# Four RMS norms of a decoder trunk take their inverse root as a power on 256 columns in GpSimd, in place of a power on 2 columns and a spreading matmul

## The chip, the cores and the metric

The kernel runs on one core of one Trainium2 chip. The metric is device time in microseconds (us). The kernel before takes 2422.91 us, the median of three runs that lie between 2422.68 and 2423.42. All times of single instructions come from one more execution, taken with the hardware profiler.

## The reference, cut to what matters

The program is a decoder trunk with two layers, 256 tokens and 2048 features, all in float32. Each layer is a token mixer, a gated MLP and an input embedding with a gate. Each of these three starts with an RMS norm, and a last norm ends the trunk: seven norms in all.

```python
def rmsnorm(x, g):
    x32 = x.astype(jnp.float32)
    y = x32 * lax.rsqrt(jnp.mean(x32 * x32, axis=-1, keepdims=True) + RMS_EPS)
    return (y * g.astype(jnp.float32)).astype(x.dtype)
...
    for i in range(DEPTH):
        a = rmsnorm(h, attn_norm[i])
...
        h = h + conv_ffn(rmsnorm(h, ffn_norm[i]), w_up[i], conv_w[i], conv_b[i], w_down[i])
        gate = jax.nn.sigmoid(rmsnorm(h, ple_norm[i]) @ w_ple_gate[i])
        h = h + gate * (p[i] @ w_ple[i])
    return rmsnorm(h, final_norm)
```

The change touches the norms with ffn_norm and ple_norm, two in each layer.

## The kernel before, in words

Activations lie with features on the 128 partitions and tokens on the 256 columns. Weights are streamed from HBM in groups of up to 1 MB (tile wr, three buffers) and cut into **units**. A unit is mostly 512 rows by 256 columns of a weight matrix. ScalarE casts it to the matmul's type (line 176) and VectorE takes the rest that the cast lost (line 177); both halves lie in one of four buffers named w. TensorE then issues 24 matmuls for the unit (line 215), each 128x256: 4 blocks of rows, 2 blocks of columns, and three products of halves. Four units make one result tile (psu, psg, pso and so on) in PSUM. The function `unit` keeps three units split ahead (LOOK = 3). As w has four buffers, the cast of unit k+4 waits until the matmuls of unit k have read theirs.

The order of the work comes from a counter. `tick` runs after each unit, and `defer(n, fn)` places a function n ticks later in the program; a scheduler then decides the order on each engine, which is fixed before the program runs. Each engine takes its instructions strictly in that order.

**The norm.** The gain of a norm is put on the activations at once (`norm_parts`), but the factor of each token, one over the root of the mean square, is put on the results of the matmuls later. So the matmuls after a norm don't wait for it. While h is completed, `norm_squares` adds up the squares of the features in a tile acc, 128 partitions by two halves of 256 tokens. `norm_finish` then defers two functions:

- `norm_sums` three ticks later: acc's two halves are added on VectorE (line 299), two matmuls with acc as weights and two columns of ones sum over the partitions (line 303, tile nps), so that the tokens come to lie on the partitions, 128 in each of two columns. VectorE divides by 2048 and adds epsilon (line 306, tile nv), and GpSimd raises the 128x2 numbers to the power -0.5 (line 308, tile rT; the exponents lie in a tile root).
- `norm_rows` five ticks later: VectorE and ScalarE each scale an identity matrix by a column of rT (lines 316 and 318, tile nd), a matmul of ones with these diagonals spreads the factors over all partitions (line 319, tile rps, 128x256), and VectorE copies them to SBUF (line 322, tile rb).

After that the factor is used: in the MLP the convolution starts with u = psu times rb (line 627 on VectorE), then comes a ScalarE instruction on u (line 630) and four VectorE instructions (line 633). In the embedding's gate it is gt = psg times rb (line 710), a sigmoid on ScalarE (line 711) and two more VectorE instructions (lines 712 and 713). `with_rows` puts these uses behind `norm_rows`. The norm in front of a mixer also needs rT itself, since the values v are scaled with tokens on the partitions, and a tile rq.

Counted from the start of the first product after a norm, TensorE's order is: units 1 to 3, nps, units 4 and 5, rps, units 6, 7, 8 and so on. Units 1 to 4 fill the first result tile, 5 to 8 the second.

Of the kernel before, what the change touches and what calls it, by code (L numbers as in the profile page):

```python
# [14 lines left out]
ALU = mybir.AluOpType  # L15
AX = mybir.AxisListType

P = 128
D = 2048
S = 256  # L20
# [10 lines left out]
EPS = 1e-6  # L31
SCALE = DH ** -0.5
# [72 lines left out]
def trunk(ctx: ExitStack, tc: tile.TileContext, xT, pT, pos, gains, conv, bf, cst, wst, out):  # L105
    nc = tc.nc
# [16 lines left out]
    acc = cpool.tile([P, 2, S], F32, name="acc")  # L123
    rb = cpool.tile([P, S], F32, name="rb")
    rq = cpool.tile([P, S], F32, name="rq")
    rT = cpool.tile([P, 2], F32, name="rT")

    root = cpool.tile([P, 2], F32, name="root")
# [3 lines left out]
    ones = ct[:, C_ONE:C_ONE + 128]  # L132

    def mm_tile(name):
        return psum.tile([P, 2, S], F32, name=name, tag="mm", bufs=4)

    def at_tile(name):
        return psum.tile([P, 2, 512], F32, name=name, tag="at", bufs=2)

    def t2_tile(name, shape=(P, 2, S), dt=F32):  # L140
        return work.tile(list(shape), dt, name=name, tag="t2", bufs=6)
# [52 lines left out]
    def defer(n, fn):  # L194
        later.append((at["tick"] + n, fn))
# [114 lines left out]
    def norm_rows(mixer):  # L310

        dg = t2_tile("nd", (P, 2, P))
        ps = at_tile("rps")
        for t in range(2):
            if t == 0:
                nc.vector.tensor_scalar_mul(out=dg[:, t, :], in0=ident, scalar1=rT[:, t:t + 1])
            else:
                nc.scalar.activation(out=dg[:, t, :], in_=ident, func=AF.Copy, scale=rT[:, t:t + 1])
        nc.tensor.matmul(ps[:, 0, :S], lhsT=ones, rhs=dg, start=True, stop=True)
        if mixer is None:  # L320
            return ps[:, 0, :S]
        nc.vector.tensor_copy(out=rb, in_=ps[:, 0, :S])
        if mixer:
            nc.vector.tensor_scalar_mul(out=rq, in0=rb, scalar1=SCALE)

    def norm_finish(mixer, sums=3, rows=5):
        at["rows"] = at["tick"] + rows
        defer(sums, norm_sums)
        defer(rows, lambda: norm_rows(mixer))

# [317 lines left out]
    for l in range(DEPTH):  # L648
        st = {}
        if l == 0:  # L650
            split_unit()
            rest_of_start()
            for op in range(8):
                if op in (2, 4, 6):
                    for i in (op - 2, op - 1):
                        norm_parts(i, 0, X)
                ple_up(0, op)
            defer(1, lambda: norm_parts(6, 0, X))
            defer(2, lambda: norm_parts(7, 0, X))
            constants()  # L660
            for i in range(8):
                defer(3 + i, lambda i=i: norm_squares(i, tc.keep_in_program_order))
            norm_finish(True, 12, 14)
# [11 lines left out]

        staggered("pso", Y, "w_out", l, _cuts(KT), out_done)
        norm_finish(False)
        for b, (g0, g1) in enumerate(BLOCKS):
            for g in range(g0, g1):
# [7 lines left out]

            staggered("psd", Y, "w_down", l, _cuts(2 * (g1 - g0)), down_done, 2 * g0, 2 * g0)
        norm_finish(False)
        if l + 1 < DEPTH:  # L690
            praw = load_p(l + 1)
# [7 lines left out]
        for op in range(8):  # L699
            end = l + 1 == DEPTH and op == 7  # L700
            if end:
                ws = [unit("w_ple_gate", l, 4 * i, op * 256)[1] for i in range(4)]
                ps = [at_tile("pse")[:, j, :S] for j in range(2)]
            else:
                ps = mm_tile("psg")
# [15 lines left out]
            else:  # L721
                more = []
                for j in range(2):
                    for k in range(KT):
                        for n, (a, b) in enumerate(((0, 0), (0, 1), (1, 0))):
                            nc.tensor.matmul(ps[j],  # L726
                                             lhsT=ws[k // 4][:, k % 4, a, j * P:(j + 1) * P],
                                             rhs=X[:, k, b, :], start=k == 0 and n == 0,
                                             stop=k == KT - 1 and n == 2)
# [14 lines left out]
    assert not later and at["unit"] == len(UNITS)  # L744
    norm_sums(more)
    rps = norm_rows(None)
    for k0, k1 in ((0, 1), (1, 2), *((k, k + 2) for k in range(2, KT, 2))):
        hs = h[:, k0:k1, :]
# [79 lines left out]
```

## Time and profile before

| what | value |
|---|---|
| three runs, median (lowest to highest) | 2422.91 us (2422.68 to 2423.42) |
| the profiled execution, its own time | 2423.48 us |
| span in its profile | 2421.7 us |
| busy share of TensorE matmuls, VectorE, ScalarE | 99%, 65%, 51% |
| busy time of GpSimd | 5.8 us in 13 instructions |
| memory traffic | 458 MB, 189 GB/s mean |

The span is what the profile covers; 1.8 us of the execution's own time lie outside of it. In a timeline row, the first number is the start in us from the beginning of the span, the second the duration of the row in all, then engine, line, operation, the tiles written and read with their shapes, the count, and in brackets how long the engine had been idle and who released it. PE is TensorE's matmuls, PEld its weight loads, DVE VectorE, ACT ScalarE, POOL GpSimd. A float32 matmul shows up as two matmul records, a fp32r one as one.

### The profile page before, as it was taken

Reading aid. Unit: us, or ns where it says so; the run is one execution under the profiler, and the core shown is the slowest. Engines: PE = TensorE matmul, PEld = TensorE weight load, DVE = VectorE, ACT = ScalarE, POOL = GpSimd, SP = SyncE. Lnnn points to the kernel's source line nnn. Section 1 sums busy time; section 2 is a strip of 40 time slices with the busy share of each in tenths; the row PEclk is TensorE's granted clock in tenths of the full one; section 3 lists DMA queues with packets and bytes.
Section 4 is the critical chain, followed back from the end, with each engine's and each line's share of the span. In section 5 each row is a group of like instructions: output and inputs, shape, how many; then the busy total and the mean of one; then the engine's idle time right before and its main releaser. Section 6 shows DMA issues by size and latency. Waiting matters only on the chain.

```text
span 2421.7 us, 47927 instructions
## 1 busy us (share of the span) xinstructions
PE 2407.1 (99%) x20992; PEld 2401.0 (99%) x20992; DVE 1581.5 (65%) x2066; ACT 1227.9 (51%) x1546; POOL 5.8 (0%) x13
## 2 busy tenths in 40 slices
PE   9999999999999999999999999999999999999998
PEld 9999999999999999999999999999999999999997
DVE  7666766776567657767755555667665776567666
ACT  6554455554355445555554444555544554455554
POOL 0000000000000000000000000000000000000000
PEclk9999999999999999999999999999999999999999
DMA  7454455555555555555555454555555555555553
GB/s 285 166 181 172 174 182 192 192 192 194 197 197 196 187 197 192 193 186 202 184 188 173 167 181 163 199 190 194 192 192 193 192 196 191 201 194 187 186 202 122
DMA packets 66818, 458.05 MB, mean 189 GB/s; under 512 B 7552, under 2 KB 7840, under 8 KB 16944
## 3 DMA queue, kind: packets, MB, share of 16 engines
q1 hardware_dynamic: 66576, 454.93, 53.3%
q8 instruction: 164, 2.69, 0.4%
q14 instruction: 46, 0.38, 0.0%
q0 software_dynamic: 32, 0.06, 0.0%
HBM read 452.86 MB, written 2.10 MB: 188 GB/s over the span
## 4 chain that ended last, share of the span: by engine, by line
PE 99%; DVE 0%; DMA 0%; ACT 0%; issue 0%; SPq 0%; POOLq 0%; DVEq 0%; ACTq 0%
PE psu L215 40%; PE psd L215 20%; PE psk L215 7%; PE psq L215 7%; PE pso L215 7%; PE psv L249 7%; PE psg L215 7%; PE avp L529 1%; PE psv L262 0%; PE psp L215 0%; PE pse L726 0%; PE scs L482 0%; PE sps L517 0%; PE avp L526 0%; DMA h<-in_x 0%; PE scs L480 0%
## 5 line engine op out<-in xcount | busy, mean ns | idle before, releaser
L177 DVE TENSOR_TENSOR w<-wr,w 128x1024 fp32r<-128x1024 f32 (+2 forms) x874 | 1045.6, 1198 | 687.2 <-ACT w L176 683.2
L176 ACT CAST w<-wr 128x1024 fp32r<-128x1024 f32 (+2 forms) x874 | 900.9, 1031 | 1065.5 <-PE psu L215 354.5
L215 PE MATMUL psu<-act,w 128*128 128x256 f32 x8448 | 959.7, 276 | 0.0
L215 PEld LDWEIGHTS psu<-act,w 128*128 128x128 f32 x8448 | 958.4, 188 | 0.1
L215 PE MATMUL psd<-act,w 128*128 128x256 f32 x4224 | 479.7, 276 | 0.0
L215 PEld LDWEIGHTS psd<-act,w 128*128 128x128 f32 x4224 | 479.2, 188 | 0.0
L215 PE MATMUL psk<-act,w 128*128 128x256 f32 x1536 | 184.3, 279 | 0.0
L215 PE MATMUL psq<-act,w 128*128 128x256 f32 x1536 | 182.6, 279 | 0.9 <-DVE w L177 0.9
L215 PEld LDWEIGHTS psk<-act,w 128*128 128x128 f32 x1536 | 179.5, 188 | 0.8
L215 PEld LDWEIGHTS psq<-act,w 128*128 128x128 f32 x1536 | 178.4, 188 | 1.7 <-DVE w L177 1.2
L215 PE MATMUL pso<-act,w 128*128 128x256 f32 x1536 | 176.5, 277 | 0.0
L215 PEld LDWEIGHTS pso<-act,w 128*128 128x128 f32 x1536 | 175.6, 188 | 0.1
L249 PE MATMUL psv<-w,act 128*128 128x256 f32 x1440 | 167.0, 277 | 0.0
L249 PEld LDWEIGHTS psv<-w,act 128*128 128x128 f32 x1440 | 165.2, 188 | 0.1
L215 PE MATMUL psg<-act,w 128*128 128x256 f32 x1440 | 164.8, 276 | 0.0
L215 PEld LDWEIGHTS psg<-act,w 128*128 128x128 f32 x1440 | 163.9, 188 | 0.1
L627 DVE TENSOR_TENSOR u<-psu,rb 128x512 f32<-128x512 f32 x88 | 60.9, 692 | 33.0 <-PE psu L215 32.8
L633 DVE SCALAR_TENSOR_TENSOR yg<-u,cv,yg 128x256 f32<-128x256 f32 x176 | 73.3, 478 | 0.0
L633 DVE SCALAR_TENSOR_TENSOR yv<-u,cv,yv 128x256 f32<-128x256 f32 x176 | 73.3, 478 | 0.0
L630 ACT ACTIVATE yg<-u,cv 128x256 f32<-128x256 f32 x88 | 48.0, 593 | 1.1 <-DVE u L627 1.1
L630 ACT ACTIVATE yv<-u,cv 128x256 f32<-128x256 f32 x88 | 48.0, 593 | 0.0
L273 ACT CAST act<-yg 128x512 fp32r<-128x512 f32 x44 | 27.3, 621 | 38.8 <-DVE yg L643 38.8
(165 smaller groups left out, 883.5 us busy)
## 6 DMA issues: line engine op xcount, KB each, us to landing
wr<-in_w SPq DMA_DIRECT2D x388, 1024.0 KB, 4.8
wr<-in_w SPq DMA_DIRECT2D x36, 768.0 KB, 4.3
wr<-in_w SPq DMA_DIRECT2D x8, 896.0 KB, 4.6
h<-in_x SPq DMA_DIRECT2D x4, 512.0 KB, 8.9
wr<-in_w SPq DMA_DIRECT2D x4, 512.0 KB, 10.0
out_dram<-h SPq DMA_DIRECT2D x7, 256.0 KB, 2.4
wr<-in_w SPq DMA_DIRECT2D x2, 816.0 KB, 4.4
pl<-in_w SPq DMA_DIRECT2D x3, 512.0 KB, 7.8
```

What stands on the lines that cost most here:

```text
L176: nc.scalar.copy(out=w[:, :, 0, :], in_=raw)
L177: nc.vector.tensor_sub(out=w[:, :, 1, :], in0=raw, in1=w[:, :, 0, :].bitcast(F32))
L215: nc.tensor.matmul(ps[:, j, :], lhsT=w[:, k, s, js], rhs=act[:, k0 - koff + k, t, :], start=first and j + k + n == 0, stop=last and k == k ...
L249: nc.tensor.matmul(ps[:, t], lhsT=act[:, 4 * i + k, a, tsl], rhs=w[:, k, b], start=i + t + k + n == 0, stop=i == 3 and k == kc - 1 and n = ...
L273: nc.scalar.copy(out=dst[:, :, 0, :], in_=src)
L529: nc.tensor.matmul(av[:, 0, j * S:(j + 1) * S], lhsT=v[:, 0, js], rhs=w[:, j * S:(j + 1) * S], start=False, stop=True, skip_group_check=True)
L627: nc.vector.tensor_mul(out=u[:, :, 2:], in0=ps, in1=rb2)
L630: nc.scalar.activation(out=y[:, j, :], in_=u[:, j, 2:], func=AF.Identity, bias=cv[:, l, t, 3:4], scale=cv[:, l, t, 2:3])
L633: nc.vector.scalar_tensor_tensor(out=y[:, j, :], in0=u[:, j, tap:tap + S], scalar=cv[:, l, t, tap:tap + 1], in1=y[:, j, :], op0=ALU.mult, ...
```

## The change

For the four norms that don't stand in front of a mixer, `norm_finish` now defers one function, `norm_wide`, by three ticks. The halves of acc are added as before. One matmul with ones as weights and acc as the moving side then gives the sums over the partitions in all 128 partitions, 128x256. VectorE divides and adds epsilon on 256 columns (tile nw), and GpSimd raises all 256 columns to the power -0.5 and writes rb itself, with the exponent column of root broadcast. The two diagonals, the matmul rps, the copy to rb, and the narrow sums nps and nv of these norms are gone. The time from which rb may be used, `at["rows"]`, is five ticks as before. The mixers' two norms and the last norm keep the old way.

```diff
+    def norm_wide():
+
+        ps = at_tile("nps")
+        nc.vector.tensor_add(out=acc[:, 0, :], in0=acc[:, 0, :], in1=acc[:, 1, :])
+        nc.tensor.matmul(ps[:, 0, :S], lhsT=ones, rhs=acc[:, 0, :], start=True, stop=True)
+        v = t2_tile("nw", (P, S))
+        nc.vector.tensor_scalar(out=v, in0=ps[:, 0, :S], scalar1=1.0 / D, scalar2=EPS,
+                                op0=ALU.mult, op1=ALU.add)
+        nc.gpsimd.tensor_tensor(out=rb, in0=v, in1=root[:, 0:1].to_broadcast([P, S]), op=ALU.pow)
 
     def norm_finish(mixer, sums=3, rows=5):
         at["rows"] = at["tick"] + rows
+        if not mixer:
+            defer(sums, norm_wide)
+            return
         defer(sums, norm_sums)
         defer(rows, lambda: norm_rows(mixer))
```

The diff also takes an `if mixer` away in `norm_rows`, which is now called for mixers and the last norm alone. All later lines stand 12 lines lower: 627 becomes 639, 630 becomes 642, 633 becomes 645.

The first of the four norms, in front of the MLP of layer 0, is the first place. The numbers behind tile names tell tiles apart. On VectorE the order before, from the division on, with w_4549, w_4592 and w_4621 the weights of units 7, 8 and 9:

```order
L306 TENSOR_SCALAR nv_4516<-nps_4512 128x2
L316 TENSOR_SCALAR nd_4576<-ct_78,rT_82 128x128
L177 TENSOR_TENSOR w_4549<-wr_4547,w_4549 128x4x256
L177 TENSOR_TENSOR w_4592<-wr_4547,w_4592 128x4x256
L322 COPY rb_80<-rps_4577 128x256
L627 TENSOR_TENSOR u_4582<-psu_4426,rb_80 128x2x256
L177 TENSOR_TENSOR w_4621<-wr_4619,w_4621 128x4x256
L633 SCALAR_TENSOR_TENSOR yg_4424<-u_4582,cv_77,yg_4424 128x256 x4
```

And VectorE in the kernel after, where w_4548, w_4585 and w_4614 are the weights of units 7, 8 and 9:

```order
L331 TENSOR_SCALAR nw_4515<-nps_4512 128x256
L177 TENSOR_TENSOR w_4548<-wr_4546,w_4548 128x4x256
L639 TENSOR_TENSOR u_4575<-psu_4426,rb_80 128x2x256
L177 TENSOR_TENSOR w_4585<-wr_4546,w_4585 128x4x256
L645 SCALAR_TENSOR_TENSOR yg_4424<-u_4575,cv_77,yg_4424 128x256 x4
L638 MEMSET u_5045 128x2x2
L177 TENSOR_TENSOR w_4614<-wr_4612,w_4614 128x4x256
```

The first use of rb, u, has moved: it stood behind the weights of unit 8 and now stands ahead of them, and unit 9's weights come behind the convolution.

The second place is the gate of layer 0, the second norm of the four, on VectorE before; w_12660, w_12703 and w_12732 are the weights of units 7, 8 and 9 there:

```order
L306 TENSOR_SCALAR nv_12627<-nps_12623 128x2
L316 TENSOR_SCALAR nd_12687<-ct_78,rT_82 128x128
L177 TENSOR_TENSOR w_12660<-wr_12658,w_12660 128x4x256
L177 TENSOR_TENSOR w_12703<-wr_12658,w_12703 128x4x256
L322 COPY rb_80<-rps_12688 128x256
L710 TENSOR_TENSOR gt_12693<-psg_12537,rb_80 128x512
L177 TENSOR_TENSOR w_12732<-wr_12730,w_12732 128x4x256
```

The same place on VectorE after, with w_12652, w_12689 and w_12718 for units 7, 8 and 9:

```order
L331 TENSOR_SCALAR nw_12619<-nps_12616 128x256
L177 TENSOR_TENSOR w_12652<-wr_12650,w_12652 128x4x256
L722 TENSOR_TENSOR gt_12679<-psg_12530,rb_80 128x512
L177 TENSOR_TENSOR w_12689<-wr_12650,w_12689 128x4x256
L724 TENSOR_TENSOR gt_12679<-gt_12679,pl_75 128x512
L725 TENSOR_TENSOR h_74<-h_74,gt_12679 128x512
L177 TENSOR_TENSOR w_12718<-wr_12716,w_12718 128x4x256
```

Here too the first use of rb, gt, now stands ahead of unit 8's weights instead of behind them.

TensorE's order at the first place after, from unit 1 to unit 9:

```order
L215 MATMUL psu_4426<-act0_70,w_4362 128x256 x24
L215 MATMUL psu_4426<-act0_70,w_4389 128x256 x24
L215 MATMUL psu_4426<-act0_70,w_4429 128x256 x24
L329 MATMUL nps_4512<-acc_79,ct_78 128x256
L215 MATMUL psu_4426<-act0_70,w_4456 128x256 x24
L215 MATMUL psu_4545<-act0_70,w_4485 128x256 x24
L215 MATMUL psu_4545<-act0_70,w_4518 128x256 x24
L215 MATMUL psu_4545<-act0_70,w_4548 128x256 x24
L215 MATMUL psu_4545<-act0_70,w_4585 128x256 x24
L215 MATMUL psu_4682<-act0_70,w_4614 128x256 x24
```

The matmul nps stands where it stood, between units 3 and 4, now as one of 128x256 instead of two of 128x2; rps, which stood between units 5 and 6, is gone.

More of the change, by code (lines that the diff above doesn't have):

```diff
@@ L322, in norm_rows @@
         nc.vector.tensor_copy(out=rb, in_=ps[:, 0, :S])
-        if mixer:
-            nc.vector.tensor_scalar_mul(out=rq, in0=rb, scalar1=SCALE)
+        nc.vector.tensor_scalar_mul(out=rq, in0=rb, scalar1=SCALE)
+    def norm_wide():
[6 more added lines that the diff above has]
+        nc.gpsimd.tensor_tensor(out=rb, in0=v, in1=root[:, 0:1].to_broadcast([P, S]), op=ALU.pow)
     def norm_finish(mixer, sums=3, rows=5):
         at["rows"] = at["tick"] + rows
+        if not mixer:
+            defer(sums, norm_wide)
+            return
         defer(sums, norm_sums)
```

## The prediction, made before the changed kernel ran

> **What bounds the kernel now.** I read the page first: busy shares, then the chain that ended last.
>
> ```profile
> PE 2407.1 (99%) x20992; PEld 2401.0 (99%) x20992; DVE 1581.5 (65%) x2066; ACT 1227.9 (51%) x1546; POOL 5.8 (0%) x13
> PE 99%; DVE 0%; DMA 0%; ACT 0%; issue 0%; SPq 0%; POOLq 0%; DVEq 0%; ACTq 0%
> ```
>
> TensorE is busy for 99% of the span, and the chain lies on it for 99%. So a change can gain only what it takes out of TensorE's own stream, and it loses when it makes TensorE wait. The waits say who is early:
>
> ```profile
> DVE w L177 <- ACT w L176: 685.0, 659, 2.6
> ACT w L176 <- PE psu L215: 354.5, 268, 1.9
> ```
>
> ScalarE waits for TensorE to give buffers of w back, and VectorE waits for ScalarE. The weights are therefore ready ahead of need, by at most the four buffers of w. That lead is what a stall on VectorE can use up before TensorE notices. How much it is, I read at the first of the four places, first from the chain there, then from the timeline of all engines:
>
> ```profile
> 398.85 8.17 PE psu L215 x72
> 407.01 0.34 PE nps L303 x4
> 407.35 5.57 PE psu L215 x48
> 412.92 0.43 PE rps L319 x2
> 413.36 2.73 PE psu L215 x24
> ```
>
> ```profile
> 407.10 1.05 ACT L176 CAST w<-wr 128x1024 fp32r<-128x1024 f32 x1 [1.66 <-PE psu L215]
> ...
> 407.39 0.16 DVE L306 TENSOR_SCALAR nv<-nps 128x2 f32<-128x2 f32 x1 [0.70 <-PE nps L303]
> 407.72 0.69 POOL L308 TENSOR_TENSOR rT<-nv,root 128x2 f32<-128x2 f32 x1 [353.04 <-DVE nv L306]
> ...
> 408.45 0.29 DVE L316 TENSOR_SCALAR nd<-ct,rT 128x128 f32<-128x128 f32 x1 [0.90 <-POOL rT L308]
> 408.65 1.21 DVE L177 TENSOR_TENSOR w<-wr,w 128x1024 fp32r<-128x1024 f32 x1
> ...
> 411.33 1.23 DVE L177 TENSOR_TENSOR w<-wr,w 128x1024 fp32r<-128x1024 f32 x1 [1.46 <-ACT w L176]
> ...
> 412.76 0.59 PE L319 MATMUL rps<-nd,ct 128*128 128x256 f32 x2
> ...
> 413.39 0.42 DVE L322 COPY rb<-rps 128x256 f32<-128x256 f32 x1 [0.84 <-PE rps L319]
> 413.85 0.69 DVE L627 TENSOR_TENSOR u<-psu,rb 128x512 f32<-128x512 f32 x1
> 414.46 1.22 DVE L177 TENSOR_TENSOR w<-wr,w 128x1024 fp32r<-128x1024 f32 x1
> ```
>
> A unit of 24 matmuls takes 2.72 us (8.17 for three). The cast at 407.10 starts when unit 3 has given its buffer back, so it is unit 7's, and the rows at 408.65, 411.33 and 414.46 finish the weights of units 7, 8 and 9.
>
> **What leaves TensorE.** Before, nps takes 0.34 us of the chain, the two units behind it 0.13 more than twice 2.72, and rps 0.43: 0.90 us per norm. After, one matmul remains with the shape of rps, which I price as rps, 0.43. So 0.47 us go per norm, and 4 x 0.47 = **1.9 us** in all. The gate's norm shows the same rows:
>
> ```profile
> 1126.01 0.34 PE nps L303 x4
> 1126.35 5.57 PE psg L215 x48
> 1131.92 0.43 PE rps L319 x2
> ```
>
> The ends of this term are a gain of nothing (a matmul of 128x256 that takes all of 0.90) and of 3.6 us (4 x 0.90, were the new one free). On VectorE nd (0.29) and the copy (0.42) go, and the division grows from 0.16 to about the 0.42 of the copy, which also reads 128x256 from PSUM; ScalarE loses a diagonal. Neither engine is on the chain, so I set these to nothing; the cover is the waiting of VectorE and ScalarE above, and without it they would be worth under half a microsecond per norm.
>
> **The new wait.** The power now stands between the sums and u. From the first matmul row of rps to the copy it takes 413.39 - 412.76 = 0.63 us, so with nps's first row at 406.85 (0.16 ahead of its place in the chain, as for rps) the division starts at 407.48 and ends at 407.90; GpSimd started 0.17 after the division's end, so the power starts at 408.07. Call its duration D. In the kernel after, VectorE finishes unit 7's weights and then waits at u for rb; behind u are queued unit 8's weights, the convolution and unit 9's weights. ScalarE stands at the convolution's first step for the same reason, with the cast of unit 9 behind it. When the power ends, u starts 0.04 later (as nd did after 408.41), unit 8's weights start 0.61 after u (414.46 - 413.85) and take 1.23: they are there 1.88 us after the power's end, at 409.95 + D. TensorE, after a norm that costs 0.43, reaches unit 8 in the chain at 407.01 + 0.43 + 4 x 2.72 = 418.32; the first matmul of a piece starts some 0.2 ahead of its place in the chain, so I take 418.1. Thus **nothing is lost up to D = 8.15 us, and each microsecond beyond is lost once per norm**. At the gates gt takes the place of u, with the same unit 8 behind it.
>
> How long is D? These are the rows that bear on it: GpSimd's only powers, its other small instruction, and two pairs of widths on VectorE.
>
> ```profile
> L308 POOL TENSOR_TENSOR rT<-nv,root 128x2 f32<-128x2 f32 x7 | 4.9, 694 | 2404.6 <-DVE nv L306 2404.6
> L129 POOL MEMSET root<- 128x2 f32 x1 | 0.1, 99 | 0.3 <-POOLq L819 0.3
> ```
>
> ```profile
> L322 DVE COPY rb<-rps 128x256 f32<-128x256 f32 x6 | 2.5, 421 | 3.4 <-PE rps L319 3.4
> L306 DVE TENSOR_SCALAR nv<-nps 128x2 f32<-128x2 f32 x7 | 1.1, 159 | 5.1 <-PE nps L303 5.1
> ```
>
> Lower end: the 0.69 us are all start, and a column costs what it does on VectorE, (0.421 - 0.159) / 254 = 0.001 us; D = 0.96. Upper end: only the 0.10 of the memset is start, and a column costs (0.69 - 0.10) / 2 = 0.296 us; D = 0.69 + 254 x 0.296 = 75.9. The break-even of 8.15 needs at most (8.15 - 0.69) / 254 = 0.029 us per column, so that 0.63 of the 0.69 us are start. The memset shows that this engine can be done with 128x2 numbers in 0.10, so about 0.6 belongs to the power itself, and I think it unlikely that nine tenths of that don't grow with the columns. Between 8.15 and 75.9, a factor of nine, I take the middle by ratio, **24 us** (0.092 per column), and keep both ends.
>
> The GPSIMD Engine Reference of the Trainium skill, section "Performance versus the Vector engine", gives 4497 ns for an addition on 2048 columns; were a power as cheap per column, an estimate from that page is 0.69 + 254 x 0.0022 = 1.25 us, and the sum would be the gain of 1.9 us alone. No row here shows an addition on GpSimd, and the page doesn't speak of powers.
>
> With D = 24 TensorE stands idle for 24 - 8.15 = 15.9 us per norm. It then starts cold, and the trace shows one such start, at the program's beginning:
>
> ```profile
> 1.19 4.63 PE L364 MATMUL idle<-act 128*128 128x256 f32 x20 [1.19 <-DVE act L361]
> ```
>
> There 20 matmuls of the usual shape took 4.63 us, 0.231 each against 2.72 / 24 = 0.113: 2.36 us lost. The ends are 0 and 2.36; I take 2.36, since that start also followed idleness. Sum per norm 15.85 + 2.36 = 18.2, times four 72.8, less 1.9: **+70.9 us**. The profiled execution took 2423.48 (span 2421.7 and 1.8 outside of it), which lies 0.57 above the median of the runs; the sum is made against it, 2494.4, and against the median it gives 2422.91 + 70.9 = **2494 us**.
>
> **The rivals.**
>
> *Hidden power.* D is below 8.15, TensorE never waits, and the time is 2422.91 - 1.9 = 2421.0. For it: on VectorE a 128x2 instruction is nearly all start. Against it: the 0.10 of the memset. It is decided at 0.029 us per column. It ends as no change: 0.2% of this kernel is 4.8 us, about what a measurement of it can tell from no change, and the gain can't exceed 3.6. Up to D = 9.8, where without a cold start 4 x 1.65 - 1.9 is 4.7, it still ends there. Chance 0.30.
>
> *VectorE held while the power runs.* If GpSimd's power blocks VectorE instructions that read two SBUF tiles, unit 7's weights, whose cast ends at 408.15, wait for it as well as u. Unit 7 is due at 415.4 and its weights come 0.04 + 1.23 after the power's end, at 409.34 + D: the loss starts at D = 6.05 instead of 8.15. With D = 24 it is 4 x (17.95 + 2.36) - 1.9 = 79.3, or 2502. No row tells: in the trace VectorE stands idle through each power, since the next instruction needs it.
>
> ```profile
>   DVE nd L316: 6.2, 7
> ```
>
> These are seven waits of nd, for seven powers. The Trainium skill has this as a rule, SBUF — State Buffer, section "Who interferes with whom": a VectorE instruction with two SBUF inputs and a GpSimd instruction that reads SBUF exclude each other for the whole instruction. By that rule the time is the 2502 of the sentences above; no run here shows it yet. Chance 0.19.
>
> *Power by the column.* D lies at 60 to 76 us, near the upper end: 4 x (60 - 8.15 + 2.36) - 1.9 = 214.9 gives 2638, and D = 75.9 gives 2701. For it: the memset's 0.10 against 0.69 for the same 128x2. Against it: a loop over many columns usually overlaps its steps, which two columns can't show. Chance 0.15.
>
> **How the numbers follow.** The forecast (D between about 9.8 and 60, only u and what is queued behind it waiting) has 0.34, the held VectorE 0.19, the power by the column 0.15: slower 0.68. Hidden 0.30 is "same". Faster by over 0.2% would need more than all of nps and rps to go, so 0.02 for what I have not seen. The forecast and the rival with a held VectorE span about 2427 to 2640 by themselves. As the hidden case has more than 0.2 it must be in the range: the low end is 2422.91 less the 3.6 at most, 2419; at the top I leave out only the power by the column, so the high end is 2640.
>
> **What the profile after would show.** One row of GpSimd per norm with 128x256 gives D at once. Right: D above 8.15, VectorE's wait at L639 and L722 put down to GpSimd, then an idle stretch of TensorE of D - 8.15 at each of the four places, ended by VectorE's w, with slower matmuls behind it, and 0.47 us less in the stream around nps. If VectorE is held, unit 7's w starts only at the power's end, and TensorE stands still one unit earlier. Wrong: D under 8, and no wait of TensorE; or a wait of u that is long while TensorE's stays short, since then the lead is longer than I count.

## The result and the profile after

The changed kernel takes 2578.34 us in the median of six runs (2564.59 to 2620.09), against 2423.62 us (2422.68 to 2425.44) for six runs of the kernel before. The ratio is **1.061, with an interval of 1.058 to 1.064**: slower by 6%, on the side that was forecast, but more than twice as far as forecast. The six runs lie on three levels, some 25 and 28 us apart: about 2565 (three runs), 2590 (one) and 2618 (two), all at a mean granted clock of 0.971 to 0.973. The ratio leaves the two runs of the highest level out. What makes the levels is part of the findings below. The profiled execution took 2620.09, with a span of 2618.3.

The page of the kernel after, the same two lines as for before:

```profile
PE 2474.6 (95%) x20976; PEld 2467.7 (94%) x20976; DVE 1580.6 (60%) x2058; ACT 1223.8 (47%) x1542; POOL 167.6 (6%) x13
PE 92%; POOL 6%; DVE 1%; ACT 0%; DMA 0%; issue 0%; SPq 0%; POOLq 0%; DVEq 0%; ACTq 0%
```

GpSimd, which had 5.8 us of work, has 167.6 and stands on the chain with 6%. And TensorE is busy for 67.5 us longer, although it has 16 records less. Both need an explanation. The group of powers gives D:

```profile
L333 POOL TENSOR_TENSOR rb<-nw,root 128x256 f32<-128x256 f32 x4 | 164.5, 41124 | 2229.4 <-DVE nw L331 2229.4
```

D is 41.12 us. The timeline at the first place shows what that does:

```profile
406.57 11.89 PE L215 MATMUL psu<-act,w 128*128 128x256 f32 x98
...
406.95 0.42 DVE L331 TENSOR_SCALAR nw<-nps 128x256 f32<-128x256 f32 x1 [0.79 <-PE nps L329]
407.46 41.13 POOL L333 TENSOR_TENSOR rb<-nw,root 128x256 f32<-128x256 f32 x1 [353.29 <-DVE nw L331]
407.65 1.50 DVE L177 TENSOR_TENSOR w<-wr,w 128x1024 fp32r<-128x1024 f32 x1 [0.28 <-ACT w L176]
...
448.62 0.69 DVE L639 TENSOR_TENSOR u<-psu,rb 128x512 f32<-128x512 f32 x1 [39.47 <-POOL rb L333]
449.23 1.22 DVE L177 TENSOR_TENSOR w<-wr,w 128x1024 fp32r<-128x1024 f32 x1
...
450.50 19.14 PE L215 MATMUL psu<-act,w 128*128 128x256 f32 x137 [32.04 <-DVE w L177]
```

VectorE splits unit 7's weights beside the power, then waits 39.47 us at u. TensorE works through units 4 to 7 and the first two matmuls of unit 8, which need only ScalarE's half of the weights (98 records), and stands still for 32.04 us, until unit 8's weights come 1.86 us after the power's end (448.59 to 450.45). The waits of TensorE give the sum over the four places:

```profile
PE psg L215 <- DVE w L177: 65.0, 2, 32.5
PE psu L215 <- DVE w L177: 64.1, 2, 32.0
```

That is 129.1 us. What follows a stall costs more. In these stretches around the first restart the last numbers are the granted clock, the DMA share and GB/s:

```profile
440.00:450.00 10.00, 0.00 (x0) 0.00 (x0) 1.38 (x2) 0.65 (x2) 8.59 (x1) 0.50 0.00 0
450.00:455.00 5.00, 4.50 (x21) 4.50 (x22) 4.01 (x8) 4.97 (x6) 0.00 (x0) 0.50 0.58 210
455.00:460.00 5.00, 5.00 (x38) 5.00 (x38) 4.97 (x8) 3.34 (x5) 0.00 (x0) 0.84 0.68 223
```

The clock is at 0.50 when TensorE restarts and for some 6 us more, which costs 4.5 x 0.50 + 5 x 0.16 = 3.0 us here. At the four restarts of this trace the granted clock stays at 0.50 for 6.1, 6.0, 4.7 and 5.2 us; at half speed that is 22.0 x 0.50 = 11.0 us lost in all. The Trainium skill, TensorE: Matmul & The Clock Gate, Part 1, states half clock after an idle window of about 3.4 us and full clock after a busy one, on windows that run freely; the halves agree, and these four lengths fit one to two such windows. (Of the eight restarts after 24 to 33 us of standing still in two runs below, the shortest stretch at 0.50 is 2.9 us, less than one window.)

The chain of the kernel after shows the rest, far from any norm: here the first MLP's up product in its second block, in the first line, and a down product.

```profile
704.84 158.29 PE psu L215 x1344
863.13 79.15 PE psd L215 x672
```

The same up product in the kernel before:

```profile
660.89 152.32 PE psu L215 x1344
```

The matmuls come every 117.78 ns instead of every 113.33, at a granted clock of 1.00 in both, with nobody waited for. This slow pace holds in this execution from the MLP norm to the next gate norm in both layers, 6336 matmuls each: 2 x 6336 x 4.45 ns = 56.4 us. The stretch behind the stall of the first gate is slow as well, 598 matmuls or 2.7 us; its row here has the restart in it too:

```profile
1232.27 73.38 PE psg L215 x598
```

So 129.1 (stalls) + 11.0 (restarts) + 56.4 + 2.7 (slow stretches) - 1.9 (sums) = 197.3, against the 2620.09 - 2423.48 = 196.6 us by which the two profiled executions differ. One slow MLP stream is worth 28.2 us, about the distance between two levels. The profiled execution is on the highest level and has both; that the lower levels lack one or both of them is inferred, since no other execution of this kernel was profiled.

The two paces aren't new. The kernel before has both within one product of its first mixer, where other short matmuls stand between the three pieces:

```profile
309.28 8.48 PE pso L215 x72
...
318.42 5.66 PE pso L215 x48
...
325.39 73.46 PE pso L215 x648
```

That is 117.8, 117.9 and 113.4 ns per matmul.

### The profile page after: what moved, and what is told of

It reads as the page before. It is cut to its first block, busy times and chain, and to the rows that moved or that the text cites. A ratio compares the mean times of both kernels' runs of the same rounds, so it can differ in the third digit from the quotient of the medians.

```text
span 2618.3 us, 47884 instructions
## 1 busy us (share of the span) xinstructions
PE 2474.6 (95%) x20976; PEld 2467.7 (94%) x20976; DVE 1580.6 (60%) x2058; ACT 1223.8 (47%) x1542; POOL 167.6 (6%) x13
## 4 chain that ended last, share of the span: by engine, by line
PE 92%; POOL 6%; DVE 1%; ACT 0%; DMA 0%; issue 0%; SPq 0%; POOLq 0%; DVEq 0%; ACTq 0%
PE psu L215 37%; PE psd L215 19%; PE psk L215 7%; PE psq L215 7%; PE pso L215 7%; POOL rb L333 6%; PE psv L249 6%; PE psg L215 6%; PE avp L541 1%; PE psv L262 0%; PE psp L215 0%; PE pse L738 0%; PE scs L494 0%; PE sps L529 0%; PE avp L538 0%; DMA h<-in_x 0%
## 5 line engine op out<-in xcount | busy, mean ns | idle before, releaser
L215 PE MATMUL psu<-act,w 128*128 128x256 f32 x8448 | 1001.4, 282 | 64.1 <-DVE w L177 64.1
L215 PEld LDWEIGHTS psu<-act,w 128*128 128x128 f32 x8448 | 1000.0, 190 | 64.6 <-DVE w L177 64.5
L215 PE MATMUL psd<-act,w 128*128 128x256 f32 x4224 | 498.5, 281 | 0.0
L215 PEld LDWEIGHTS psd<-act,w 128*128 128x128 f32 x4224 | 497.9, 189 | 0.0
L333 POOL TENSOR_TENSOR rb<-nw,root 128x256 f32<-128x256 f32 x4 | 164.5, 41124 | 2229.4 <-DVE nw L331 2229.4
L215 PE MATMUL psg<-act,w 128*128 128x256 f32 x1440 | 173.3, 284 | 65.0 <-DVE w L177 65.0
L215 PEld LDWEIGHTS psg<-act,w 128*128 128x128 f32 x1440 | 172.3, 194 | 65.5 <-DVE w L177 65.4
L722 DVE TENSOR_TENSOR gt<-psg,rb 128x512 f32<-128x512 f32 x15 | 10.4, 691 | 84.2 <-POOL rb L333 78.9
```

Source lines behind the costliest of these rows:

```text
L215: nc.tensor.matmul(ps[:, j, :], lhsT=w[:, k, s, js], rhs=act[:, k0 - koff + k, t, :], start=first and j + k + n == 0, stop=last and k == k ...
L333: nc.gpsimd.tensor_tensor(out=rb, in0=v, in1=root[:, 0:1].to_broadcast([P, S]), op=ALU.pow)
L722: nc.vector.tensor_mul(out=gt, in0=ps, in1=rb2)
```

## The experiments

Theory after the result: the loss is the stall of D - 8.15 per norm, with D growing by the column, plus the restarts. That a slower pace of the matmul stream adds to it, which each MLP may or may not fall into, entered only with the fifth run; the expectations of the first four don't have it. Rivals: the wide form or GpSimd as such is slow; VectorE can't work beside the power; the slow pace comes from the stall, from GpSimd, or from the matmuls that were exchanged. Times of a group were taken beside runs of the kernel before of 2422.88 us (the first four), 2423.62 (the next four) and 2423.7 (the last four) in the median.

**A multiplication in place of the power.**

```diff
+    nil = cpool.tile([P, 2], F32, name="nil")
+    nc.gpsimd.memset(nil, 0.0)
...
-        nc.gpsimd.tensor_tensor(out=rb, in0=v, in1=root[:, 0:1].to_broadcast([P, S]), op=ALU.pow)
+        nc.gpsimd.tensor_tensor(out=rb, in0=v, in1=nil[:, 0:1].to_broadcast([P, S]), op=ALU.mult)
```

> GpSimd multiplies the 256 columns by zero in place of the power, so the four norms' factor is 0 and no longer the root. If the 41.12 us are the power's own, a multiplication on 256 columns takes 1 to 2 us, VectorE's u and gt don't wait for it long enough to matter, TensorE never stands still at the four places, and the time is that of before less the 1.9 us of the sums, about 2421.7. If 256 columns are slow on GpSimd whatever the operation, or if the wide sums or the order on VectorE are what costs, TensorE stands still for some 32 us per norm here too and the time is about 2565.

Measured: 2477.50 us, ratio 1.0226 (1.0210 to 1.0241). GpSimd's group:

```profile
L335 POOL TENSOR_TENSOR rb<-nw,nil 128x256 f32<-128x256 f32 x4 | 2.5, 615 | 2240.8 <-DVE nw L333 2240.8
```

0.61 us on 256 columns: it is the power that is slow, not GpSimd or the width. TensorE doesn't stand still at the four places. Yet the time is 54.6 us above before, not 1.9 below. Neither side of the expectation had that: both MLP streams run at the slow pace, and 56.4 - 1.9 = 54.5.

**The power on 32 and on 64 columns.** The edit, here for 32 columns:

```diff
+        nc.gpsimd.tensor_tensor(out=rb[:, :32], in0=v[:, :32], in1=root[:, 0:1].to_broadcast([P, 32]), op=ALU.pow)
```

> The power runs on the first 32 of the 256 columns only; the other columns of rb keep older factors. If the power costs a start of 0.37 and 0.159 us per column (41.12 for 256, 0.69 for 2), it takes 5.5 us here, below the break-even of 8.15, so TensorE never waits and the time is about 1.9 us below before. If the wide form has a fixed price of tens of microseconds, the time stays near 2565.

> The power runs on the first 64 columns only. By 0.37 and 0.159 us per column it takes 10.5 us, 2.4 over the break-even: TensorE stands still 2.4 us per norm, and the time is 4 x 2.4 - 1.9 = 7.7 us above before if so short a stop restarts at full speed, up to 22 above if each restart costs the 3.5 us that the kernel after seems to pay. If the break-even were one unit earlier, 6.05, because VectorE is held by the power, the stop would be 4.5 us per norm and the time 16 us above before without a restart's price.

Measured: 2478.98 us for 32 columns, ratio 1.0232 (1.0217 to 1.0247), and 2487.38 for 64, ratio 1.0266 (1.0251 to 1.0282). The powers, first of 32 columns, then of 64:

```profile
L333 POOL TENSOR_TENSOR rb<-nw,root 128x32 f32<-128x32 f32 x4 | 21.7, 5418 | 2231.3 <-DVE nw L331 2231.3
```

```profile
L333 POOL TENSOR_TENSOR rb<-nw,root 128x64 f32<-128x64 f32 x4 | 42.1, 10523 | 2224.8 <-DVE nw L331 2224.8
```

With 41.12 for 256 columns, a column costs (10.52 - 5.42) / 32 = 0.159 and (41.12 - 10.52) / 192 = 0.159 us; 0.3 to 0.4 us is start. The 32 columns are hidden; with 64, TensorE stands still 1.5 us at an MLP norm and 1.9 at a gate:

```profile
PE psg L215 <- DVE w L177: 3.8, 2, 1.9
PE psu L215 <- DVE w L177: 2.9, 2, 1.5
```

This sum is 6.7 us, 1.7 per norm where 2.4 was expected; the two kernels differ by 8.4. Both lie 57 to 58 us above what was expected of them (for 64 columns, without a price for the restart), again with both MLP streams slow.

**The first use of rb later, at the gates alone.**

```diff
-        norm_finish(False)
+        norm_finish(False, rows=8)
...
-                nc.vector.tensor_mul(out=gt, in0=ps, in1=rb2)
+                place = tc.keep_in_program_order if op == 0 else (lambda ins: ins)
+                place(nc.vector.tensor_mul(out=gt, in0=ps, in1=rb2))
```

> All 256 columns, but at the two gates the first use of rb comes behind the weights of units 8, 9 and 10 on VectorE instead of ahead of unit 8's; the two MLP norms are as in the kernel after. If the loss is set by what stands behind the first use of rb, TensorE stops three units later at the gates, so its idle time there falls by 3 x 2.72 = 8.2 us, from 32.5 to 24.3, while at the MLP norms it stays at 32; the time falls by 16 us against the kernel after. If VectorE can't work beside the power, these weights aren't split in time and nothing falls.

Measured: 2573.43 us (2547.03 to 2577.88), ratio 1.0585 (1.0529 to 1.0642). TensorE's waits:

```profile
PE psu L215 <- DVE w L177: 64.1, 2, 32.0
PE psg L215 <- DVE w L177: 48.0, 2, 24.3
```

The gates' stalls fall from 32.5 to 24.3 us, by the three units that were put ahead of the use, and the MLP norms' don't. So the loss is set by what is queued on VectorE behind the first use of rb. The median fell by 4.9 us only, not by the 16 expected, as the time falls on levels again; the lowest run, 2547.03, is 18 below the lowest one of the kernel after. While the power of 41.12 us that starts at 1191.95 runs, VectorE splits four units:

```profile
1192.08 1.57 DVE L177 TENSOR_TENSOR w<-wr,w 128x1024 fp32r<-128x1024 f32 x1 [0.27 <-ACT w L176]
...
1195.22 1.23 DVE L177 TENSOR_TENSOR w<-wr,w 128x1024 fp32r<-128x1024 f32 x1 [1.57 <-ACT w L176]
...
1197.94 1.23 DVE L177 TENSOR_TENSOR w<-wr,w 128x1024 fp32r<-128x1024 f32 x1 [1.49 <-ACT w L176]
```

Three of them take the usual 1.23 us (two are shown), only the one that starts with the power takes 0.3 longer. VectorE isn't held.

**The wide sums without GpSimd.** To find where the 56 us are from, the root is taken in another way.

```diff
-        nc.gpsimd.tensor_tensor(out=rb, in0=v, in1=root[:, 0:1].to_broadcast([P, S]), op=ALU.pow)
+        nc.vector.reciprocal(out=v, in_=v)
+        nc.scalar.activation(out=rb, in_=v, func=AF.Sqrt)
```

> The wide sums stay, but the root is taken by a reciprocal on VectorE and a square root on ScalarE instead of GpSimd's power. Theory: with the stall gone, what is left of the loss is that TensorE's stream runs at 117.8 ns per matmul instead of 113.3 from the wide sums of an MLP norm up to the next gate norm: 2 x 6336 x 4.45 ns = 56 us, less the 1.9 us of the sums, so about 2477, as in the two runs with a short or cheap GpSimd instruction. Rival: the slow stream comes from GpSimd's instruction or from the wait on it; then it is gone here, and the time is about 2421.

Measured: 2478.20 us, ratio 1.0223 (1.0208 to 1.0239). No GpSimd, no stall, and still 54.6 us above before. In the chain, the three units ahead of the sums and the stream behind them:

```profile
398.70 8.16 PE psu L215 x72
407.30 172.43 PE psu L215 x1464
```

72 matmuls at 113.3 ns ahead, 1464 at 117.8 behind: the pace changes at the new matmul.

All edits below take the root in this way too, but for the kernel before with an extra matmul and the last run, which keep their powers; the diffs leave these lines out.

**The sums behind unit 5.**

```diff
-        norm_finish(False)
+        norm_finish(False, 5, 6)
```

> As the run with reciprocal and square root, but the wide sums stand behind unit 5 instead of unit 3, where the spreading matmul of the same shape stood before, and rb is used from six ticks on. If the place in the stream decides whether the slow pace sets in, the stream stays at 113.3 ns and the time is about 2421 to 2422; if every single wide matmul at the head of the MLP brings it, about 2477.

Measured: 2477.35 us, ratio 1.0221 (1.0206 to 1.0236).

```profile
398.16 13.60 PE psu L215 x120
412.19 166.77 PE psu L215 x1416
```

Five units at 113.3 ns ahead of the sums, then 117.8. The place doesn't matter: the same shape at the place where the spreading matmul stood without harm brings the slow pace.

**The kernel before with an extra wide matmul**, at the two MLP norms, behind the narrow sums:

```diff
+    def extra():
+        ps = at_tile("xps")
+        nc.tensor.matmul(ps[:, 0, :S], lhsT=ones, rhs=acc[:, 0, :], start=True, stop=True)
...
         norm_finish(False)
+        defer(3, extra)
```

> The kernel before, with one matmul more per MLP norm, two in all: ones times acc, 128x256, right behind the narrow sums, its result unused. Work added: 2 x 0.43 us. If the wide matmul sets the slow pace and nothing resets it, the time is 56 us above before, about 2479; if the spreading matmul two units later resets it, only some 2 x 48 matmuls are slow, and the time is about 1.3 us above before.

Measured: 2424.58 us, ratio 1.0005 (0.9995 to 1.0014): no difference. So a wide matmul doesn't bring the slow pace by itself when the narrow sums stand ahead of it. The 48 matmuls directly behind it, ahead of the spreading matmul, are fast already, so it isn't the spreading matmul that resets the pace:

```profile
406.90 0.54 PE xps L333 x2
407.44 5.46 PE psu L215 x48
...
413.33 160.49 PE psu L215 x1416
```

**The wide matmul twice**, second result unused:

```diff
         nc.tensor.matmul(ps[:, 0, :S], lhsT=ones, rhs=acc[:, 0, :], start=True, stop=True)
+        nc.tensor.matmul(ps[:, 1, :S], lhsT=ones, rhs=acc[:, 0, :], start=True, stop=True)
```

> As the run with reciprocal and square root, with the wide matmul issued twice in a row at all four norms, the second result unused; 4 x 0.24 us more of work. If it is the number of passes that puts the stream out of step (the narrow sums had four passes and didn't, the wide ones have two), four passes leave it at 113.3 ns and the time is about 2422; if any wide float32 matmul at this place does, it is about 2478.

Measured: 2480.47 us, ratio 1.0234 (1.0218 to 1.0249), streams slow. The number of passes, which show up as matmul records, isn't it.

**The narrow sums ahead of the wide ones**, as a mere spacer:

```diff
+        for t in range(2):
+            nc.tensor.matmul(ps[:, 1, 2 * t:2 * t + 2], lhsT=acc[:, 0, t * P:(t + 1) * P],
+                             rhs=ones[:, 0:2], start=True, stop=True)
         nc.tensor.matmul(ps[:, 0, :S], lhsT=ones, rhs=acc[:, 0, :], start=True, stop=True)
```

> As the run with reciprocal and square root, with the two narrow matmuls of 128x2 put back ahead of the wide one at all four norms, their results unused. Theory: a lone wide float32 matmul puts a stream of 113.3 ns per matmul into the slow pace, and one that follows the narrow ones directly doesn't, as in the kernel before with an extra wide matmul. Then the MLP streams stay at 113.3 ns and the time is that of before less about 0.4 us per norm for the spreading matmul, plus nothing else: 2422 to 2423. If the slow pace belongs to the wide sums as such, or to the missing spreading matmul two units later, it is about 2479.

Measured: 2423.35 us, ratio 0.9998 (0.9990 to 1.0007): the 55 us are gone, by two matmuls whose results nobody reads.

```profile
401.29 8.17 PE psu L215 x72
...
409.80 0.54 PE nps L332 x2
410.34 165.94 PE psu L215 x1464
```

The stream stays at 113.3 ns, without a spreading matmul, so it isn't the lack of that one either that brings the slow pace. This is also the best version of the wide sums that I found, and it isn't measurably faster than the kernel before.

**The wide sums at the gates alone**, with reciprocal and square root; the edit makes `norm_wide` depend on a flag that only the gates set.

```diff
-        norm_finish(False)
+        norm_finish(False, wide=True)
```

> The wide sums, with reciprocal and square root, at the two gate norms alone; the MLP norms are as in the kernel before. In the other runs the stream came into the gate norm slow and left it fast; here it comes in fast. If a lone wide matmul turns a fast stream slow here too, some 1300 matmuls behind the two gates are slow, 1300 x 4.45 ns = 5.8 us, less 2 x 0.47 for the sums: 4.8 us above before, 2428. If the MLP streams alone are concerned, the time is 0.9 us below before.

Measured: 2429.66 us, ratio 1.0027 (1.0016 to 1.0037), 6.0 above before, with 4.8 expected for the slow case.

```profile
1118.14 8.16 PE psg L215 x72
1126.30 0.43 PE nps L330 x2
1126.73 81.97 PE psg L215 x696
```

So a fast stream goes slow here as well. In the other runs a slow stream came into the gate and left it fast. In the one with reciprocal and square root at all four norms it takes 117.8 ns per matmul ahead of the sums and 113.4 behind:

```profile
1145.05 8.48 PE psg L215 x72
...
1153.97 78.91 PE psg L215 x696
```

So the wide matmul doesn't slow a stream down, it switches the pace.

**The narrow sums behind the wide ones.** The lines of the spacer stand behind the wide matmul.

> As the run with reciprocal and square root, with the two narrow matmuls behind the wide one instead of ahead of it. If what counts is that the last matmuls ahead of the stream are narrow ones, the stream stays fast, 2422 to 2423; if the wide one has set the pace already and narrow ones leave it, 2479.

Measured: 2479.50 us, ratio 1.0232 (1.0218 to 1.0245), slow. Narrow matmuls guard the pace only from ahead.

**The kernel after, with the spacer ahead of its sums.**

> The kernel after with its power, and the two narrow matmuls ahead of the wide one, results unused. The four stalls stay: 4 x (32.2 + 3.5) us. If the slow stretches of the kernel after come from the wide sums and only end by chance in a stall, all runs lie near 2424 + 143 = 2567. If the restart after a stall sets the pace by chance, the runs scatter from 2567 to 2623 as before, in steps of 28 us.

Measured: 2580.44 us (2567.81 to 2593.36), ratio 1.0648 (1.0610 to 1.0686): three runs near 2568, three near 2593. In the profiled one, at the first norm:

```profile
406.81 11.47 PE L215 MATMUL psu<-act,w 128*128 128x256 f32 x98
451.66 18.62 PE L215 MATMUL psu<-act,w 128*128 128x256 f32 x142 [33.38 <-DVE w L177]
```

The 98 records between sums and stall take 11.47 us, against 11.89 in the kernel after: the spacer kept the pace. Behind the stall that stream is slow (158.29 for 1344 matmuls), and the second layer's is fast (152.32). So a restart after a long stall sets the pace anew, and not always to the same: of the twelve restarts after 24 to 33 us in the three profiled kernels that have them, six came out slow and six fast. This execution, of the level near 2593, has one slow MLP stream.

## Why the prediction was wrong

**The bound and the wait: right.** TensorE's stream was the bound, VectorE's in-order wait at the first use of rb was the new wait, and unit 8's weights were the first thing missing. The break-even of 8.15 us gives 41.12 - 8.15 = 33.0 us per norm; 32.0 and 32.5 were measured. From the power's end to unit 8's weights it takes 1.86 us, against 1.88 worked out.

**The step that failed: "I take the middle by ratio, 24 us".** D is 41.12. I had bounded the start of the power from below by the 0.10 of the memset; the start is 0.3 to 0.4 of the 0.69, and the rest grows with the columns, 0.159 us each. With D = 41.12 the sum of the prediction gives 4 x (32.97 + 2.36) - 1.9 = 139.4, that is 2562, next to the lowest level of 2565. That one term is the whole distance from 2494 to there, 68 of the 84 us by which the median of 2578 lies above the forecast. (The middle by ratio of 8.15 and 75.9 is 24.9, not 24; that slip is 3.5 us of the sum.)

**A term that was missing: the price of the exchange itself.** "What leaves TensorE" counted the matmuls that go and come, 1.9 us, and took the rest of the stream as given. The exchange of two narrow matmuls and a later wide one for a lone wide one changes the pace of up to 6336 matmuls behind it, by 28 us per layer. In the six kernels whose wide sums have no narrow ones ahead of them at any of the four norms, and no stall, the time lies 54 to 57 us above before. In the kernel after, the stall's restart sets the pace again; 0, 28 or 56 us fit its levels, and 56 is what its one profile shows. I had named no rival for a change of pace. The term was put at nothing without a reason, although the kernel before has both paces in its mixer. That 2578 lies below the upper end of 2640 is no merit of the sum: the range had room for a D of up to 60, not for a change of pace.

**The restart** costs 2.4 to 3.1 us in the kernel after, against the 2.36 assumed, from half a clock for 4.7 to 6.1 us. That the price came near is partly luck: it was taken from the program's start, where the profile shows a granted clock of 1.00, so that nothing shows the two to be the same event.

**The rivals.** *Hidden power* fell: D is five times the break-even, and even a hidden one ends at 2479, as the run with 32 columns shows. *VectorE held* fell: instructions with two SBUF inputs take their usual 1.23 us within the power's 41; the rule of the Trainium skill, SBUF — State Buffer, section "Who interferes with whom", is not what this chip did with a power. *Power by the column* had the mechanism, with too small a start and so too high a price. The estimate from the GPSIMD Engine Reference of the Trainium skill, section "Performance versus the Vector engine", holds for an instruction of the kind that the page prices: 256 x 0.0022 = 0.56 us by its addition, against 0.61 for the multiplication; it says nothing of a power.

**Still open:** why a lone wide matmul switches the pace, and why narrow ones directly ahead of it prevent that; and what decides the pace at a restart. In the traces, a wide matmul at one of the four norms with no narrow one ahead of it switched the pace in 38 of 38 cases, from fast to slow or from slow to fast, and one with the narrow sums directly ahead kept it in 10 of 10. With the narrow sums two units ahead, the spreading matmuls of the kernel before kept it too, but one in the first mixer of the run with the multiplication did not: the 48 matmuls ahead of it are fast, and those behind it take 117.7 ns each.

```profile
60.28 5.65 PE psq L217 x48
```

So what the runs give is a rule of this kernel's streams, not a mechanism.

## What to carry to other kernels

A single measured duration on two columns says nothing of how it splits into start and columns; measure the instruction at the width that is meant, alone, before it goes on an in-order engine ahead of work that others wait for. The lead of the engine that feeds the bound, counted in units and read from the timeline, told the stall to a microsecond. And after any exchange of instructions in a long matmul stream, compare the time per matmul far behind the edit: the pace itself can change. Ahead of an edit, look whether the same matmuls already run at two paces somewhere in the kernel.

## What the runs showed of the hardware that I had not expected

- GpSimd's power costs 0.159 us per column of 128 numbers and 0.3 to 0.4 us of start, whereas its multiplication of 128x256 takes 0.61 us in all.
- The same stream of 128x256 matmuls with the same granted clock of 1.00 has two paces, 113.33 and 117.78 ns per matmul, each stable for over 700 us; interruptions by matmuls of another shape, or a stop of 24 to 33 us, can switch it, either way. The stops of 1.5 us in the run with 64 columns didn't end the slow pace.
